# Experts' columns in blocks of 1024, a token's weight applied when a result is added to it, and another order of the products in a piece

## The chip, the core and the metric

The kernel runs on one core of a Trainium2 chip. The metric is device time in microseconds (us), the median of several runs. TensorE (PE) multiplies, ScalarE (ACT) and VectorE (DVE) evacuate PSUM and prepare operands, SyncE (SP) issues the loads. Times with five or six digits in the rows below are places in the profiled execution, counted from its start.

## The reference

The program is a two-layer encoder on 256 tokens of 1024 columns. Each layer is a mixer and then a feed-forward part; in the second layer that part is a mixture of eight experts of width 3584. The change touches the experts alone:

```python
def swiglu(h, w1, w3, w2):
    return (jax.nn.silu(h @ w1) * (h @ w3)) @ w2

def moe_swiglu(h, router_w, w1, w3, w2):
    t = h.reshape(B * L, D)
    logits = (t @ router_w).astype(jnp.float32)
    top_val, top_idx = lax.top_k(logits, TOP_K)
    top_w = jax.nn.softmax(top_val, axis=-1)
    combine = jnp.einsum('tk,tke->te', top_w, jax.nn.one_hot(top_idx, N_EXPERTS))
    out = jnp.zeros_like(t)
    for e in range(N_EXPERTS):
        out = out + combine[:, e:e + 1] * swiglu(t, w1[e], w3[e], w2[e])
    return out.reshape(B, L, D)
```

## The kernel before

Every float32 product is made of float32r products. A weight piece r (4 KB a partition, 512 KB in all, one load on SP's queue) is split into H, a copy by ACT (L319, tile wh), and L = r - H, a subtraction by DVE (L320, tile wl); activations are split in the same way. A product then takes three matrix products: high times H, high times L, low times H. H and L have four slots each. When PE takes a piece (`take`), the split of the piece three further on is put into the queues of ACT and DVE, where it waits until PE has done with the slot. Loaded pieces wait in some twenty further tiles.

The experts run one after the other. At most 128 tokens of an expert are gathered by products with a one-hot matrix (tiles gx). The 3584 columns of w1 and w3 are worked in seven blocks of 512. A block is, in PE's order: the product with w1 (L1884 to L1886, 24 matrix products into one PSUM tile `mo`), the transposes of the former block's activations (L1844, PSUM tile `maT`), the product with w3 (24), and the former block's product with w2 (L1813 to L1815, 24, into two PSUM tiles `my`). Behind that, ACT computes the block's Silu from w1's tile (L1894) and DVE multiplies by w3's tile (L1895). PE, ACT and DVE all work in the order in which the program issues (`by_hand`).

PSUM has eight tiles of one bank: four with the tag `pw` (all of `mo`), two `pg` (`my`) and two `pl` (transposes, gathers, scatters). Tiles of a tag are handed out in turn, and a tile's next writer waits until the readers of its former content are done.

When the last block of an expert is through w2, its result is scaled by the tokens' weights (`weighted`: ACT L1822 writes ywH, DVE L1823 writes ywL); the weights in slot order (`wsl`) come from products of the one-hot matrix (L1799). `scatter` brings the result back to token order in four units of two products (L1836, L1837, PSUM tile `sc`), each added to the sum by DVE (L1838). Scatter and gather are issued between the rows of the running products: a call of `pump` lets a waiting unit go when its count is down.

A piece of w1 or w3 holds two rows of 128 by 512 columns (2 KB runs in memory); a piece of w2 holds one row of 1024 columns (4 KB runs).

Of the kernel before, what the change touches and what calls it, by code (L numbers as in the profile page):

```python
# [10 lines left out]
F32 = mybir.dt.float32  # L11
# [4 lines left out]
OP = mybir.AluOpType  # L16
# [16 lines left out]
def _constants():  # L33
    """Masks and identities, all set by the shapes alone."""
# [43 lines left out]
def _build(ctx, tc, nc, A, out, dbg, upto):  # L78
# [6 lines left out]
    # a pool for all phases (tags m..), and two (tags g.. and l..) of the mixers that the experts' replace  # L85
# [19 lines left out]
    # slots of a pool's tags; the last character of a tag is its size: 4, 2, 1 KB, h(alf), s(mall)  # L105
# [14 lines left out]
    # work that is issued between the pieces of a long product  # L120
# [41 lines left out]
    # ------------------------------------------------------------------ constants and small inputs  # L162
# [70 lines left out]
    # rotary angles: the argument reduced to [-pi, pi], cos from the half angle  # L233
# [26 lines left out]
    # lambda of the differential attention, and rows that depend on parameters alone  # L260
# [28 lines left out]
    # the slots of the weights' pieces: the pools that hold them, each with its number  # L289
# [14 lines left out]
    # instructions of a critical chain, behind which the engines' other work is queued  # L304
# [8 lines left out]
    def split(r, early=None, lows=None):  # L313
        """Two float32r parts whose sum is r, in the slots of the weights or of another tag."""
# [42 lines left out]
    def load_ahead(tags):  # L357
        """The next pieces of the plan, into tiles of their own tags (or the weights' slots)."""
# [5 lines left out]
    def lend(until):  # L364
        """The tiles of the pieces loaded ahead also hold later pieces, in the same order, up to the until-th piece."""
# [19 lines left out]
    def pieces(name, rows, step=1, k=0, ahead=True):  # L385
        """(k, H, L) over the contraction, from row k; work of the sides is issued every step rows."""
# [7 lines left out]
    def mm_nat(o, k, H, L, xs, tb, last, parts=(0, 1)):  # L394
        """Activations stationary: [128 tokens, columns] += ."""
# [7 lines left out]
    def proj_nat(name, xs, rows=KD, n=512):  # L403
        """[tokens, n] for both token blocks."""
# [6 lines left out]
    def proj_first(name, xs, stages):  # L411
        """proj_nat of the first block: token block 1 becomes ready after token block 0."""
# [14 lines left out]
    def proj_T(name, n, xs, step=1, o=None, k0=0, rows=KD):  # L427
        """[n columns, 256 tokens] in chunks of 128 columns, two to a bank; k0, rows: a part of the contraction."""
# [35 lines left out]
    def adaln(todo, every):  # L464
        """Vectors (layer, index) of the modulation as columns [128, 8], a piece of the weights at a time."""
# [11 lines left out]
    def sums(half):  # L477
        """Columns half * 4.. of the modulation's first two vectors: pieces on PE or on DVE, and the end."""
# [107 lines left out]
    def row_of(col, name):  # L586
        """A [128, 8] column vector as a row of 1024 on every partition."""
# [9 lines left out]
    def norm_T(l, n_i, sc_i, sh_i, keep=None):  # L597
        """The modulated norm of x, transposed, as two float32r parts [128, 2, 8, 128]: tiles, and a step a block."""
# [19 lines left out]
        def xn(tb, at=512):  # L618
            """Scaled on DVE as far as column at, beyond on ACT."""
# [16 lines left out]
        def hf(tb, q, dve=2):  # L636
            """The first columns on DVE, the others on ACT."""
# [18 lines left out]
    def warm(n):  # L656
        """Products that nothing reads, to keep PE's clock up while it waits for a chain of other engines."""
# [5 lines left out]
    def rstd2(ss, name):  # L663
        """(ss[:, 0] + ss[:, 1] + eps) ** -0.5, of squares that were divided by 1024"""
# [5 lines left out]
    def to_T(src_cols, ks, dst, scale=None, tags=("pl",)):  # L670
        """Transposed, scaled by a column and split: src_cols(tb, k) -> [128 tokens, 128]; dst = (H, L). In steps."""
# [18 lines left out]
    def residual(ys):  # L690
        """The steps of x += g * rmsnorm(y); ys[tb] are the halves of y, [128, 512] each."""
# [28 lines left out]
    def transition(r, grow, n, then):  # L720
        """The residual r, and the norm n as far as block 0's transposes and then(), in the order in which the data comes."""
# [21 lines left out]
    def after(res, norm):  # L743
        """The steps of a norm that follows a residual, for a product that begins with token block 0."""
# [1276 lines left out]
```

## Time and profile before

| what | us |
|---|---|
| median of three timed runs | 1929.86 |
| lowest and highest of them | 1929.14, 1938.19 |
| span of the profiled execution, first to last instruction | 1935.8 |
| PE busy | 1886.1 (97%) |
| DVE busy | 1598.8 (83%) |
| ACT busy | 1329.8 (69%) |

The page lists no time of the profiled execution besides its span, which lies among the three timed runs. Matrix products overlap in the records: a product of 512 columns is listed with about 0.39 us, but one starts every 0.23 us; the distance of starts is what counts. The experts run from 933.7 us to the end.

### The profile page before, as it was taken

The numbers are of one execution on the slowest core, as the hardware profiler recorded it, in microseconds if no ns is written. First come the engines' busy times: TensorE is split into PE (matmuls) and PEld (weight loads), VectorE is DVE, ScalarE is ACT, GpSimd is POOL, SyncE is SP. The second block draws the span as 40 slices with busy tenths as digits, with TensorE's granted clock in tenths as the row PEclk, the third lists the DMA queues.
The fourth block names the chain that finished last, engine by engine and source line by source line (L and its number), as shares of the span: only waits on it lengthen the run. The fifth ranks groups of instructions, "written<-read, shape, count | busy, mean of one in ns | idle before, by whom it ended". The sixth has DMA issues, their size and how long they took to land.

```text
span 1935.8 us, 32487 instructions
## 1 busy us (share of the span) xinstructions
PE 1886.1 (97%) x12232; PEld 1583.8 (82%) x12232; DVE 1598.8 (83%) x1993; ACT 1329.8 (69%) x1874; POOL 30.1 (2%) x54
## 2 busy tenths in 40 slices
PE   7999999999999999999999999999999999999997
PEld 6987788799878878787788888888888888888885
DVE  6887876677756887766899988999889999899997
ACT  4785566643346873665777787777887778877775
POOL 1000000000000000000000000000000000000000
PEclk9999999999999999999999999999999999999999
DMA  9545755478874557558799999999999999999992
GB/s 326 162 129 174 221 175 182 154 251 268 283 227 125 148 155 219 185 184 322 267 342 351 337 349 344 367 370 356 355 338 369 369 354 368 335 358 373 360 322 107
DMA packets 258018, 531.30 MB, mean 274 GB/s; under 512 B 22126, under 2 KB 45116, under 8 KB 257852
## 3 DMA queue, kind: packets, MB, share of 16 engines
q1 hardware_dynamic: 257500, 528.99, 79.7%
q8 instruction: 98, 1.61, 0.3%
q14 instruction: 68, 0.56, 0.1%
q0 software_dynamic: 192, 0.07, 0.0%
q10 hardware_dynamic: 160, 0.07, 0.0%
HBM read 528.02 MB, written 1.05 MB: 273 GB/s over the span
## 4 chain that ended last, share of the span: by engine, by line
PE 75%; DMA 9%; DVE 6%; ACT 6%; issue 2%; SPq 1%; POOL 0%; DVEq 0%; ACTq 0%; POOLq 0%
PE mo L1884 11%; PE mo L1886 11%; PE mo L1885 11%; PE my L1813 5%; PE my L1814 5%; PE my L1815 5%; DMA raw<-in_adaln_w 4%; PE pn L398 4%; PE pn L401 4%; PE pn L399 4%; DMA raw<-in_ffn_w 2%; DVE wl L320 2%; ACT wh L319 2%; PE pt L437 2%; PE pt L438 2%
## 5 line engine op out<-in xcount | busy, mean ns | idle before, releaser
L320 DVE TENSOR_TENSOR wl<-raw,wh 128x1024 fp32r<-128x1024 f32 (+1 forms) x893 | 1076.3, 1222 | 166.3 <-ACT wh L319 126.8
L319 ACT CAST wh<-raw 128x1024 fp32r<-128x1024 f32 (+1 forms) x893 | 931.8, 1053 | 380.0 <-PE mo L1886 96.9
L1884 PE MATMUL mo<-wh,gx 128*128 128x512 f32 x896 | 357.0, 398 | 0.0
L1885 PE MATMUL mo<-wl,gx 128*128 128x512 f32 x896 | 351.0, 392 | 0.0
L1886 PE MATMUL mo<-wh,gx 128*128 128x512 f32 x896 | 350.9, 392 | 0.0
L1886 PEld LDWEIGHTS mo<-wh,gx 128*128 128x128 f32 x896 | 168.2, 188 | 38.6 <-ACT gx L1785 1.2
L1884 PEld LDWEIGHTS mo<-wh,gx 128*128 128x128 f32 x896 | 168.4, 188 | 34.7 <-ACT gx L1785 0.6
L1885 PEld LDWEIGHTS mo<-wl,gx 128*128 128x128 f32 x896 | 168.5, 188 | 34.5 <-DVE wl L320 0.2
L1813 PE MATMUL my<-wh,aTm 128*128 128x512 f32 x448 | 175.9, 393 | 0.0
L1814 PE MATMUL my<-wl,aTm 128*128 128x512 f32 x448 | 175.3, 391 | 0.0
L1815 PE MATMUL my<-wh,aTm 128*128 128x512 f32 x448 | 175.1, 391 | 0.0
L437 PE MATMUL pt<-xH,wh 128*128 128x256 f32 x576 | 165.7, 288 | 0.0
L438 PE MATMUL pt<-xH,wl 128*128 128x256 f32 x576 | 163.1, 283 | 2.1 <-DVE wl L320 2.1
L439 PE MATMUL pt<-xL,wh 128*128 128x256 f32 x576 | 162.9, 283 | 0.0
L398 PE MATMUL pn<-wh,xH 128*128 128x512 f32 x352 | 150.0, 426 | 0.0
L401 PE MATMUL pn<-wh,xL 128*128 128x512 f32 x352 | 139.4, 396 | 0.0
L399 PE MATMUL pn<-wl,xH 128*128 128x512 f32 x352 | 139.4, 396 | 0.0
L450 DVE SCALAR_TENSOR_TENSOR acc<-raw,scol,acc 128x512 f32<-128x512 f32 x140 | 104.7, 748 | 39.9 <-DMA raw<-in_adaln_w 38.0
L438 PEld LDWEIGHTS pt<-xH,wl 128*128 128x128 f32 x576 | 110.4, 192 | 2.8 <-DVE wl L320 2.5
L437 PEld LDWEIGHTS pt<-xH,wh 128*128 128x128 f32 x576 | 110.4, 192 | 0.3
L439 PEld LDWEIGHTS pt<-xL,wh 128*128 128x128 f32 x576 | 110.4, 192 | 0.0
L1815 PEld LDWEIGHTS my<-wh,aTm 128*128 128x128 f32 x448 | 84.1, 188 | 18.9
(450 smaller groups left out, 2518.2 us busy)
## 6 DMA issues: line engine op xcount, KB each, us to landing
raw<-in_moe_w SPq DMA_DIRECT2D x672, 512.0 KB, 5.3
raw<-in_w_in SPq DMA_DIRECT2D x128, 512.0 KB, 3.8
raw<-in_adaln_w SPq DMA_DIRECT2D x80, 512.0 KB, 4.6
raw<-in_ffn_w SPq DMA_DIRECT2D x66, 512.0 KB, 4.8
raw<-in_w_branch SPq DMA_DIRECT2D x24, 512.0 KB, 4.2
rawe<-in_adaln_w SPq DMA_DIRECT2D x16, 512.0 KB, 7.9
raw<-in_w_out SPq DMA_DIRECT2D x16, 512.0 KB, 4.9
x<-in_x SPq DMA_DIRECT2D x2, 512.0 KB, 6.9
```

What stands on the lines that cost most here:

```text
L319: S.copy(H, r)
L320: low = lambda: tt(L, r, H, op=OP.subtract)
L398: mm(o, xH[:, tb, k, :], H, start=k == 0, stop=False)
L437: mm(d, H[:, cs], xH[:, :, k, :], start=k == 0 and c % 2 == 0, stop=False, skip_group_check=True)
L438: mm(d, L[:, cs], xH[:, :, k, :], start=False, stop=False, skip_group_check=True)
L439: mm(d, H[:, cs], xL[:, :, k, :], start=False, stop=k == KD - 1, skip_group_check=True)
L1813: mm(y[hf], aT[:, 0, k, :], H[:, c], start=b == 0 and k == 0, stop=False)
L1814: mm(y[hf], aT[:, 0, k, :], L[:, c], start=False, stop=False)
L1815: mm(y[hf], aT[:, 1, k, :], H[:, c], start=False, stop=b == nb - 1 and k == 3)
L1884: mm(q, gH[:, k, :], H, start=k == 0, stop=False)
L1885: mm(q, gH[:, k, :], L, start=False, stop=False)
L1886: mm(q, gL[:, k, :], H, start=False, stop=k == KD - 1)
```

## The change

Blocks are now 1024 columns wide (three of 1024 and one of 512 per expert). A piece of w1 or w3 is one row of 1024 columns. A block's w1 and w3 take two PSUM tiles each, and within a piece the order is: high and low times H for the first half, high and low times H for the second, then high times L for both. `turned` transposes two tiles, `gated` computes two Silus and two products. `parted` splits the result without weights; the weight is a column operand of the addition, which becomes a SCALAR_TENSOR_TENSOR, and the products for `wsl` are gone. `pump` is called once per row and half. The numbers that say how long the lent tiles hold loaded pieces (`lend`) follow the new order.

```diff
+    EB = [(c, min(1024, DE - c)) for c in range(0, DE, 1024)]
...
-        nb = DE // 512
+        nb = len(EB)
...
-                ws = ps("ws", [P, 2])
...
-                        mm(ws[:, j:j + 1], hot[tb][:, j, :].bitcast(F32), combk[:, tb, e:e + 1],
-                           start=tb == 0, stop=tb == 1)
...
-                    act(yH[:, c], y[hf], AF.Copy, scale=wcol)
-                    stt(yL[:, c], y[hf], wcol, yH[:, c], op0=OP.mult, op1=OP.subtract)
+                    S.copy(yH[:, c], y[hf])
+                    tt(yL[:, c], y[hf], yH[:, c], op=OP.subtract)
...
-                        tt(acc[tb][:, c], acc[tb][:, c], o, op=OP.add)
+                        stt(acc[tb][:, c], o, combk[:, tb, e:e + 1], acc[tb][:, c], op0=OP.mult, op1=OP.add)
...
-                        q = ps("mo", [P, 512], "pw")
+                        o[w] = [ps("mo", [P, 512], "pw") for _ in subs]
...
-                                mm(q, gH[:, k, :], H, start=k == 0, stop=False)
-                                mm(q, gH[:, k, :], L, start=False, stop=False)
-                                mm(q, gL[:, k, :], H, start=False, stop=k == KD - 1)
-                                pump()
+                                for q, j in zip(o[w], subs):
+                                    c = slice(512 * j, 512 * j + 512)
+                                    mm(q, gH[:, k, :], H[:, c], start=k == 0, stop=False)
+                                    mm(q, gL[:, k, :], H[:, c], start=False, stop=False)
+                                for q, j in zip(o[w], subs):
+                                    c = slice(512 * j, 512 * j + 512)
+                                    mm(q, gH[:, k, :], L[:, c], start=False, stop=k == KD - 1)
+                                    pump()
...
                     def gated():
-                        act(t, o[0], AF.Silu)
-                        tt(t, t, o[1], op=OP.mult)
+                        for j in subs:
+                            act(t[j], o["moe_w1"][j], AF.Silu)
+                            tt(t[j], t[j], o["moe_w3"][j], op=OP.mult)
```

Three places show how the change moves instructions. The first is ACT's queue where expert 0's result is complete, behind the first block of expert 1. `my_1` and `my_2` are the result's halves, `mo` the PSUM tiles of the block's w1. Before:

```order
L319 CAST wh_316_11367<-raw1_5_9924 128x1024
L1822 ACTIVATE ywH_1_11377<-my_1_10417,wsl_1_10147 128x512
L1822 ACTIVATE ywH_1_11377<-my_2_10418,wsl_1_10147 128x512
L1894 ACTIVATE ma_8_11330<-mo_15_11224 128x512
L319 CAST wh_317_11387<-raw1_6_9926 128x1024
```

And now:

```order
L319 CAST wh_324_11455<-raw_383_11453 128x1024
L1821 CAST ywH_1_11465<-my_1_10602 128x512
L1821 CAST ywH_1_11465<-my_2_10603 128x512
L1901 ACTIVATE ma_8_11415<-mo_15_11217 128x512
L1901 ACTIVATE ma_9_11416<-mo_16_11218 128x512
L319 CAST wh_325_11479<-raw_384_11477 128x1024
```

There are two Silus instead of one, behind the same two copies. `mo_15` and `mo_16` are the w1 tiles of this block, `mo_17` and `mo_18` its w3 tiles; with four `pw` tiles handed out in turn, the next block's w1 tiles, `mo_19` and `mo_20`, take the places of `mo_15` and `mo_16`. Before, one block took two tiles and the next block's w1 the places of the block before the last.

The second place is PE's queue in the w1 product of the following block, at the scatter of expert 0 (`sc_18` and `sc_19` are its second and third unit, `maT_8` and `maT_9` the transposes of the former block):

```order
L1893 MATMUL mo_19_11475<-wl_328_11516,gx_3_10144 128x512
L1834 MATMUL sc_18_11564<-ywH_1_11465,hT_1_10146 128x512
L1835 MATMUL sc_18_11564<-ywL_1_11466,hT_1_10146 128x512
L1893 MATMUL mo_20_11476<-wl_328_11516,gx_3_10144 128x512
...
L1893 MATMUL mo_19_11475<-wl_329_11528,gx_3_10144 128x512
L1834 MATMUL sc_19_11580<-ywH_1_11465,hT_1_10146 128x512
L1835 MATMUL sc_19_11580<-ywL_1_11466,hT_1_10146 128x512
L1893 MATMUL mo_20_11476<-wl_329_11528,gx_3_10144 128x512
L1844 MATMUL maT_8_11585<-cc_79,ma_8_11415 128x128 x4
L1844 MATMUL maT_9_11593<-cc_79,ma_9_11416 128x128 x4
```

Three of the four scatter units now stand ahead of the transposes, and the transposes fill two `pl` tiles, those that `sc_18` and `sc_19` held. Before, all four units stood behind the transposes, which filled one tile.

The third is DVE's queue at the same place, with the additions of those units (`acc`) between the subtractions (`wl`):

```order
L320 TENSOR_TENSOR wl_330_11540<-raw_389_11537,wh_330_11539 128x1024
L1836 SCALAR_TENSOR_TENSOR acc_25_11008<-sc_17_11548,combk_9931,acc_25_11008 128x512
L320 TENSOR_TENSOR wl_331_11556<-raw_390_11553,wh_331_11555 128x1024
L1836 SCALAR_TENSOR_TENSOR acc_25_11008<-sc_18_11564,combk_9931,acc_25_11008 128x512
L320 TENSOR_TENSOR wl_332_11572<-raw_391_11569,wh_332_11571 128x1024
L1836 SCALAR_TENSOR_TENSOR acc_26_11009<-sc_19_11580,combk_9931,acc_26_11009 128x512
L1847 TENSOR_TENSOR aTm_8_11590<-maT_8_11585,aTm_8_11590 128x512
L1847 TENSOR_TENSOR aTm_9_11598<-maT_9_11593,aTm_9_11598 128x512
```

The addition that frees `sc_19` for `maT_9` stands behind two subtractions and two other additions that begin after the first unit.

## Rows read from the trace of the kernel before

**Rows 1.** Busy time by stage: us, PE PEld DVE ACT POOL, clock, DMA share, GB/s.

```profile
500.00:600.00 100.00, 91.65 (x447) 74.30 (x446) 64.02 (x83) 47.45 (x69) 3.12 (x6) 0.98 0.68 217
...
1200.00:1300.00 100.00, 100.00 (x450) 82.00 (x449) 93.38 (x86) 77.69 (x82) 0.00 (x0) 1.00 1.01 365
...
1500.00:1600.00 100.00, 100.00 (x450) 81.92 (x449) 93.44 (x88) 78.61 (x84) 0.00 (x0) 1.00 0.99 362
```

**Rows 2.** Waits from 950 to 1920 us: us in total, times, longest.

```profile
ACT wh L319 <- PE mo L1886: 96.2, 285, 0.8
...
DVE wl L320 <- DMA raw<-in_moe_w: 9.3, 35, 1.2
...
ACT wh L319 <- DMA raw<-in_moe_w: 1.6, 5, 0.3
...
PEld mo L1885 <- DVE wl L320: 0.2, 1, 0.2
```

**Rows 3.** Timeline at the border of two blocks: start, us, engine, line.

```profile
1246.66 0.39 PE L1815 MATMUL my<-wh,aTm 128*128 128x512 f32 x1
...
1247.08 1.05 ACT L319 CAST wh<-raw 128x1024 fp32r<-128x1024 f32 x1 [0.31 <-PE my L1815]
...
1248.02 0.39 PE L1815 MATMUL my<-wh,aTm 128*128 128x512 f32 x1
1248.04 0.59 ACT L1894 ACTIVATE ma<-mo 128x512 f32<-128x512 f32 x1
1248.24 0.40 PE L1884 MATMUL mo<-wh,gx 128*128 128x512 f32 x1
...
1248.53 1.04 ACT L319 CAST wh<-raw 128x1024 fp32r<-128x1024 f32 x1
...
1251.03 0.39 PE L1884 MATMUL mo<-wh,gx 128*128 128x512 f32 x1
...
1253.52 0.39 PE L1886 MATMUL mo<-wh,gx 128*128 128x512 f32 x1
```

**Rows 4.** Timeline where an expert's result is complete.

```profile
1315.88 0.39 PE L1815 MATMUL my<-wh,aTm 128*128 128x512 f32 x1
1315.91 1.26 ACT L1822 ACTIVATE ywH<-my,wsl 128x512 fp32r<-128x512 f32 x2
1316.11 0.40 PE L1884 MATMUL mo<-wh,gx 128*128 128x512 f32 x1
...
1317.06 0.59 ACT L1894 ACTIVATE ma<-mo 128x512 f32<-128x512 f32 x1
```

**Rows 5.** Timeline at the end: additions free PSUM tiles that PE waits for.

```profile
1921.75 1.36 DVE L1838 TENSOR_TENSOR acc<-acc,sc 128x512 f32<-128x512 f32 x2
...
1922.49 0.50 PE L1836 MATMUL sc<-ywH,hT 128*128 128x512 f32 x1
...
1922.83 0.40 PE L1837 MATMUL sc<-ywL,hT 128*128 128x512 f32 x1
```

**Rows 6.** ACT's timeline at the first Silu.

```profile
949.50 1.03 ACT L319 CAST wh<-raw 128x1024 fp32r<-128x1024 f32 x1
950.55 1.28 ACT L1894 ACT_TABLE_LOAD   x1
951.84 0.60 ACT L1894 ACTIVATE ma<-mo 128x512 f32<-128x512 f32 x1
```

**Rows 7.** Groups from 950 to 1900 us: busy us, mean ns, idle before.

```profile
L320 DVE TENSOR_TENSOR wl<-raw,wh 128x1024 fp32r<-128x1024 f32 x650 | 781.2, 1222 | 72.5 <-ACT wh L319 36.9 <-DMA raw<-in_moe_w 9.3
...
L1823 DVE SCALAR_TENSOR_TENSOR ywL<-my,wsl,ywH 128x512 fp32r<-128x512 f32 x14 | 9.8, 743 | 0.0
...
L1799 PE MATMUL ws<-combk,hot 128*128 128x1 f32 x32 | 4.0, 229 | 0.0
```

**Rows 8.** The chain that ended last: start, us, what.

```profile
1253.91 0.44 PE maT L1844 x4
...
1414.62 0.34 PE ws L1799 x4
```

**Rows 9.** PE's timeline in the first layer's feed-forward part.

```profile
575.22 0.40 PE L1503 MATMUL po<-wh,gT 128*128 128x512 f32 x1
...
577.79 0.39 PE L1505 MATMUL po<-wh,gT 128*128 128x512 f32 x1
```

More of the change, by code (lines that the diff above doesn't have):

```diff
@@ L1804, in gather, with parted @@
                     S.copy(hT[j], o[:, j])
-                S.copy(wsl, ws)
             def down(y, b, aT, then=None):
-                for k, H, L in pieces("moe_w2", 4):
+                rows = EB[b][1] // P
+                for k, H, L in pieces("moe_w2", rows):
                     if k == 1 and then:
                         then()
+                    a = aT[k // 4][:, :, k % 4, :]
                     for hf in range(2):
                         c = slice(hf * 512, hf * 512 + 512)
-                        mm(y[hf], aT[:, 0, k, :], H[:, c], start=b == 0 and k == 0, stop=False)
-                        mm(y[hf], aT[:, 0, k, :], L[:, c], start=False, stop=False)
-                        mm(y[hf], aT[:, 1, k, :], H[:, c], start=False, stop=b == nb - 1 and k == 3)
-            def weighted(y, wcol):
+                        mm(y[hf], a[:, 0], H[:, c], start=b == 0 and k == 0, stop=False)
+                        mm(y[hf], a[:, 0], L[:, c], start=False, stop=False)
+                        mm(y[hf], a[:, 1], H[:, c], start=False, stop=b == nb - 1 and k == rows - 1)
+            def parted(y):
                 yH = tl("ywH", [P, D], "m4", F32R)
@@ L1832, in scatter, with turned @@
                         o = ps("sc", [P, 512])
-                        for e in es:
-                            yH, yL = yws.pop(e) if hf == tb == 1 else yws[e]
-                            hT = of[e][1]
-                            mm(o, hT[:, tb, :], yH[:, c], start=e == es[0], stop=False)
-                            mm(o, hT[:, tb, :], yL[:, c], start=False, stop=e == es[-1])
-                        tt(acc[tb][:, c], acc[tb][:, c], o, op=OP.add)
-            def turned(t):
-                q = ps("maT", [P, 4, P])
-                for k in range(4):
-                    nc.tensor.transpose(q[:, k, :], t[:, k * P:k * P + P], ident)
-                aT = tl("aTm", [P, 2, 4, P], "m4", F32R)
-                S.copy(aT[:, 0], q)
-                tt(aT[:, 1], q, aT[:, 0], op=OP.subtract)
-                return aT
+                        yH, yL = yws.pop(e) if hf == tb == 1 else yws[e]
+                        hT = of[e][1]
+                        mm(o, hT[:, tb, :], yH[:, c], start=True, stop=False)
+                        mm(o, hT[:, tb, :], yL[:, c], start=False, stop=True)
+                        stt(acc[tb][:, c], o, combk[:, tb, e:e + 1], acc[tb][:, c], op0=OP.mult, op1=OP.add)
+            def turned(ts_):
+                aTs = []
+                for t in ts_:
+                    q = ps("maT", [P, 4, P])
+                    for k in range(4):
+                        nc.tensor.transpose(q[:, k, :], t[:, k * P:k * P + P], ident)
+                    aT = tl("aTm", [P, 2, 4, P], "m4", F32R)
+                    S.copy(aT[:, 0], q)
+                    tt(aT[:, 1], q, aT[:, 0], op=OP.subtract)
+                    aTs.append(aT)
+                return aTs
             def end(e, b, aT, every, then=None):
@@ L1855, in end @@
                 if b == nb - 1:
-                    yws[e] = weighted(ys[e], of[e][2])
-                    return Side(scatter((e,), every), 1)
+                    yws[e] = parted(ys[e])
+                    return Side(scatter(e, every), 1)
             of, ys, yws, prev = {}, {}, {}, None
@@ L1863, in experts @@
                 for b in range(nb):
-                    if e % 2 and b == 4 and e + 1 < NE:
+                    if e % 2 and b == 2 and e + 1 < NE:
                         more = Side(gather(e // 2 + 1, 4), 1)
@@ L1867, in experts @@
                         more.drain("gather")
-                    if not acc and b == 5:
+                    if not acc and b == nb - 1:
                         acc.extend(tl("acc", [P, D], "l4") for _ in range(2))
@@ L1871, in experts @@
                             G.memset(t, 0.0)
-                    o = []
                     final = e == NE - 1 and b == nb - 1
+                    subs = range(EB[b][1] // 512)
+                    o = {}
                     for w in ("moe_w1", "moe_w3"):
-                        q = ps("mo", [P, 512], "pw")
-                        for k0 in range(0, KD, 2):
-                            if e == b == 0 and w == "moe_w1":
+                        o[w] = [ps("mo", [P, 512], "pw") for _ in subs]
+                        k = -1
+                        while k < KD - 1:
+                            if e == b == 0 and w == "moe_w1" and k % 2:
@@ L1878, in experts @@
                                 next(first)
                                 next(first)
-                                if k0 == KD - 2:
+                                if k == KD - 3:
                                     Side(first, 8)
                             gH, gL = of[e][0]
-                            for k, H, L in take(w, not (final and w == "moe_w3" and k0 >= KD - 4)):
-                                mm(q, gH[:, k, :], H, start=k == 0, stop=False)
-                                mm(q, gH[:, k, :], L, start=False, stop=False)
-                                mm(q, gL[:, k, :], H, start=False, stop=k == KD - 1)
-                                pump()
@@ L1888, in experts @@
-                        o.append(q)
+                            for k, H, L in take(w, not (final and w == "moe_w3" and k >= KD - 5)):
+                                for q, j in zip(o[w], subs):
[6 more added lines that the diff above has]
+                                    pump()
@@ L1900, in experts @@
                         gated()
-                    if e == NE - 1 and b == nb - 3:
+                    if e == NE - 1 and b == nb - 2:
                         grow = row_of(gcol, "grow")
```

18 lines of the change are left out of this document (8 added, 10 removed).

## The prediction

> **What bounds the kernel now.** I read the busy time by stage first. The change touches only the experts, from 933.7 us on. There PE is busy for all of every 100 us at full clock, DVE for 93, ACT for 79, and the DMA engines for about all of it; in the first layer's feed-forward part, which the change leaves alone, PE has gaps [rows 1]. Three resources are near their limit, so the waits decide which one sets the pace. In the whole stage PE waited 0.2 us for a split piece, while ACT waited 96 us for PE to give a slot back; the loads kept DVE waiting 9.3 us and ACT 1.6 [rows 2]. ACT and DVE follow PE. PE's queue is the path: whatever adds a wait to PE is added to the time, and a faster load, copy or addition gives nothing as long as PE does not wait for it.
>
> What PE's path is made of is seen at a border of two blocks [rows 3]. A product starts every 0.23 us: 12 products from 1248.24 to 1251.03 take 2.79 us, the next 11 take 2.49, or 0.2264 each. So a new product runs 12 x 0.2264 = 2.72 us worth of work in 2.79, that is 0.07 us is lost at its start, and the rest goes at one spacing whichever operand is stationary.
>
> **The change, part by part.**
>
> *Wider rows in memory.* The 8 x 7 x 12 = 672 pieces stay 512 KB each. The page has no row for 4 KB runs alone. Upper bound of the gain: everything that was waited for a load, 9.3 + 1.6 = 10.9 us, if it lay on PE's path; lower bound 0. It lies on DVE and ACT, who are ahead of PE, so I take 0. The cover is PE's own work; if PE became faster the loads would be next, at 0.99 to 1.01 of the DMA engines' time [rows 1]. The Trainium skill ("Perfetto Trace Analysis", DMA Optimizations) says that larger transfers, 4 KB in place of 2 KB, can raise throughput much where DMA is the limit; the DMA share would agree, the waits do not.
>
> *The products.* Their number is the same, 8 x 7 x 72 = 4032 in all, 2688 of them of w1 and w3, and so is that of the transposes. An expert starts 12 products (w1, w3, w2 in four blocks) instead of 21; 8 x 9 x 0.07 = 5.0 us less. Bounds: 0, if the loss comes back with the alternation of two PSUM tiles; or a slower spacing throughout, as in the feed-forward part, where 11 steps from 575.22 to 577.79 take 0.2336 each [rows 9]. Against the mean of the first 23 steps here, (2.79 + 2.49) / 23 = 0.2296, that is 0.004 on 2688 products of w1 and w3, 10.8 us more. I take 5.0 less, since new products are nearest to what both stages show.
>
> *The weights' products.* 4 pairs of experts, two groups each of 0.34 us on the chain [rows 8], all 32 records of the group [rows 7]: 4 x 2 x 0.34 = 2.7 us less, on PE's path. Bounds 0 (if the transposes next to them wait as long anyway) and 2.7.
>
> *A wait at the border of blocks.* This is the main term. All four `pw` tiles are now one block's; the next block's first product needs the tile that the Silu reads, and the Silu stands in ACT's queue behind w2's product. Today the Silu starts at 1248.04, because the copy before it starts only when PE gives a slot back (1247.08, after the product of 1246.66), and ends at 1248.63; PE's next product starts at 1248.24 and needs nothing from it [rows 3]. Now it must wait. What such a wait costs beyond the reader's end is seen at the end of the kernel: the addition ends at 1921.75 + 0.68 = 1922.43, the product that needs its tile starts at 1922.49, and the following one 0.34 later instead of 0.23 [rows 5]. So: 1248.63 + 0.06 - 1248.24 + 0.11 = 0.56 us. The second Silu ends 0.49 later (the distance from the first to the copy behind it, 1248.04 to 1248.53), and its tile is needed two products, 0.57 us, after the first: no second wait. The tiles turn so that the border from the 512 block to the next expert is free; two borders per expert (second and third block, third and fourth) cost this: 16 x 0.56 = 9.0 us. Bounds: 0.39, the bare overlap, to 0.62: 6.2 to 9.9.
>
> *The border at which an expert's result is complete.* Between an expert's first and second block ACT first copies the former expert's result, so the Silu starts only at 1317.06 and ends at 1317.65, while PE goes on at 1316.11 [rows 4]. The wait is 1.54 + 0.06 + 0.11 = 1.71 us, for experts 1 to 7: 12.0 us. Bounds: 1.54 to 1.8, 10.8 to 12.6. For expert 0 the table load, 1.28, and the Silu, 0.60, follow a copy of 1.03 [rows 6]; that copy starts about when PE begins its last row of 6 products (1.38 us) and the wait is 1.03 + 1.28 + 0.60 - 0.2 - 1.38 + 0.17 = 1.5 us; bounds 0 and 1.5. The 0.2 is that H is now given back two products earlier, so that the copy three rows ahead starts 0.2 to 0.3 before PE begins a row. This extra lead of ACT and DVE is all that the order within a piece gives; as PE did not wait for them, it is worth 0.
>
> *The transposes behind the scatter.* `maT_9` takes the tile of the third scatter unit. Count from PE's start on the row with the first unit. PE needs three rows of 6 products and three units of 2, 24 x 0.228, and four transposes of 0.44 in all [rows 8]: it wants the tile at 5.9. DVE ends the subtraction ahead of the first addition at about 2.1 (copy from -0.25 to 0.8, then 1.22 [rows 7]); then come addition, subtraction, addition, subtraction, addition. An addition with a weight does not exist before; nearest is the same operation with a PSUM input, 0.74 [rows 7]. So 2.1 + 3 x 0.74 + 2 x 1.22 = 6.8, and with the 0.06 and 0.11 a wait of 1.1 us, for 7 experts 7.7 us. Bounds 0, if DVE is ahead, and 1.5, if it comes late out of the double block of multiplications: 0 to 10.5. Queued behind `maT_9` on PE is the whole of w3; nothing else waits.
>
> *The rest.* Two multiplications and two transposed copies come at once on DVE and ACT instead of one; the lead of the splits covers them, and PE's new waits lengthen it. The additions are 0.06 longer on DVE, 28 of them off PE's path; four at the end cost 0.2, and the plain copies of the result give about as much back. Zero.
>
> *Sum*: 9.0 + 12.0 + 1.5 + 7.7 - 5.0 - 2.7 = 22.5 us more. On the profiled execution, 1935.8, that is 1958.3; this execution is 5.9 above the median of the three runs, so for a median I predict 1929.9 + 22.5 = 1952 us.
>
> The Trainium skill ("Perfetto Trace Analysis", Optimizing Tensor Performance, Matmuls) asks that independent products rotate through different PSUM banks, so that reading one overlaps the next. The kernel before does so, the trace agrees (the 1248.24 product needs no reader), and the change gives it up: by the rule slower, as in the sum.
>
> **The rivals.**
>
> *The waits do not show.* If ACT reached the Silus before PE is through w2, the three wait terms vanish and 5.0 + 2.7 are left: 1922 us, within 0.5%. For it: ACT has 21 of 100 us free. Against: the order puts the Silu behind a copy that PE itself releases in the last row but one.
>
> *Products get closer.* The new order seldom repeats a stationary operand. If that took the spacing of w1's and w3's products from 0.2296 to 512 columns at 2.4 GHz (the granted clock is 1.00), 0.2133, it would give 2688 x 0.0163 = 43.8 us, in place of the 5.0: 1929.9 + 27.5 - 43.8 = 1914 us, faster. It decides from 0.014 us a product. Against: in the 2.49 us of equal steps the stationary operand changes at two of three steps and stays at the third, with no difference. The Trainium skill ("TensorE: Matmul & The Clock Gate", Back-to-back issue gap) gives 0.216 us for 512 columns; no row here shows that.
>
> *Loads were the bound after all.* All 10.9 us come back, the waits stay: 1941 us, 0.6% slower.
>
> **How the numbers follow.** 0.5% is 9.6 us, about what a measurement of this kernel can tell from no change. The forecast's case, 1940 to 1966, has 0.70; the waits hidden wholly or mostly, 1922 to 1939, 0.18; closer products 0.09; loads 0.03, mostly just slower. Faster 0.10, same 0.19, slower 0.71. The terms' own bounds: at least 6.2 + 10.8 - 5.0 - 2.7 = 9, at most 9.9 + 12.6 + 1.5 + 10.5 + 10.8 - 2.7 = 43. The range 1930 to 1966 leaves out the closer products, the lower half of the hidden waits, and the top of the last sum.
>
> **What would show it.** In the profile after, PE's idle time or the distance of starts at the first w1 product of a block should name the Silu's line: 0.4 to 0.6 us at 16 places, 1.6 to 1.8 at 7; the transposes behind a scatter should wait about 1 us for an addition; starts inside a product should keep 0.226 to 0.235. The prediction is wrong if PE runs through those borders, or if the spacing inside w1 and w3 moves by over 0.005.

## The result, and the profile after

The changed kernel takes 1954.32 us (median of 4 runs, 1953.64 to 1956.04) against 1929.5 us for the kernel before (median of 4 runs, 1929.13 to 1938.19): ratio 1.0115, 95% interval 1.0092 to 1.0139 (the quotient of the two medians, 1.0129, lies inside it). It is slower, and within 3 us of the forecast.

Busy time by stage in the changed kernel (PE, its loads of stationary operands as PEld, DVE, ACT, POOL, clock, DMA share, GB/s), which answers to [rows 1]:

```profile
1200.00:1300.00 100.00, 97.90 (x436) 79.18 (x435) 91.11 (x85) 76.34 (x81) 0.00 (x0) 1.00 0.96 354
1500.00:1600.00 100.00, 98.19 (x441) 79.83 (x440) 90.97 (x85) 76.39 (x82) 0.00 (x0) 1.00 0.97 362
```

PE, full before, now idles for 2 of every 100 us at the same clock, and DVE, ACT and the loads all do a little less per 100 us. Nobody is fuller than before: a wait has been added. Its name stands in the waits from 950 to 1935 us (us in total, times, longest), as in [rows 2]:

```profile
ACT wh L319 <- PE mo L1890: 92.3, 285, 0.8
...
PEld mo L1889 <- ACT ma L1901: 28.2, 40, 2.2
...
PE mo L1889 <- ACT ma L1901: 15.1, 24, 1.8
...
DVE wl L320 <- DMA raw<-in_moe_w: 11.8, 45, 1.2
ACT wh L319 <- DMA raw<-in_moe_w: 3.8, 12, 0.3
PEld maT L1844 <- DVE acc L1836: 3.6, 7, 0.5
...
PE maT L1844 <- DVE acc L1836: 2.0, 7, 0.3
```

L1889 is the first product of a row's half of w1 or w3, L1901 the Silu, L1836 the scatter's addition. PE waits for the Silu at 24 places, which are all the borders that the prediction counted (16, 7 and 1), and for the addition at 7. The totals of PE are too small (a product's record is listed longer than the distance of starts), so the sizes below are taken from starts. The timeline at an ordinary border, which answers to [rows 3]:

```profile
1242.55 1.06 ACT L319 CAST wh<-raw 128x1024 fp32r<-128x1024 f32 x1 [0.30 <-PE my L1814]
1243.51 1.08 ACT L1901 ACTIVATE ma<-mo 128x512 f32<-128x512 f32 x2
...
1243.49 0.39 PE L1814 MATMUL my<-wh,aTm 128*128 128x512 f32 x1
1244.15 0.50 PE L1889 MATMUL mo<-wh,gx 128*128 128x512 f32 x1 [0.28 <-ACT ma L1901]
1244.49 0.40 PE L1890 MATMUL mo<-wh,gx 128*128 128x512 f32 x1
```

The first of the two Silus begins at 1243.51 behind a copy that PE released late, and ends some 0.59 later, at 1244.10. PE starts at 1244.15, 0.66 after w2's last product instead of 0.227, and the next product follows 0.34 later, as in [rows 5]. The border behind which an expert's result is complete, which answers to [rows 4]:

```profile
1329.41 1.07 ACT L1821 CAST ywH<-my 128x512 fp32r<-128x512 f32 x2
1330.36 1.10 ACT L1901 ACTIVATE ma<-mo 128x512 f32<-128x512 f32 x2
...
1329.39 0.39 PE L1814 MATMUL my<-wh,aTm 128*128 128x512 f32 x1
1331.03 0.50 PE L1889 MATMUL mo<-wh,gx 128*128 128x512 f32 x1 [1.25 <-ACT ma L1901]
```

Here the two copies go first, and PE loses 1.64 - 0.23 = 1.41 and 0.1 behind it. Expert 0's first border, which answers to [rows 6]:

```profile
953.46 2.01 ACT L319 CAST wh<-raw 128x1024 fp32r<-128x1024 f32 x2
955.49 1.28 ACT L1901 ACT_TABLE_LOAD   x1
956.78 1.09 ACT L1901 ACTIVATE ma<-mo 128x512 f32<-128x512 f32 x2
...
957.43 0.50 PE L1889 MATMUL mo<-wh,gx 128*128 128x512 f32 x1 [1.81 <-ACT ma L1901]
```

PE's product ahead of it starts at 955.23, so 2.20 - 0.23 = 1.97 us are lost here.

The second transposes behind the additions of a scatter:

```profile
1341.83 0.75 DVE L1836 SCALAR_TENSOR_TENSOR acc<-sc,combk,acc 128x512 f32<-128x512 f32 x1
1342.49 1.22 DVE L320 TENSOR_TENSOR wl<-raw,wh 128x1024 fp32r<-128x1024 f32 x1
1343.63 0.74 DVE L1836 SCALAR_TENSOR_TENSOR acc<-sc,combk,acc 128x512 f32<-128x512 f32 x1
...
1343.54 0.60 PE L1844 MATMUL maT<-cc,ma 128*128 128x128 f32 x4
1344.42 0.66 PE L1844 MATMUL maT<-cc,ma 128*128 128x128 f32 x4 [0.28 <-DVE acc L1836]
```

The third addition ends at 1344.37, and the tile's transposes start at 1344.42 instead of 1343.98.

Because the stages ahead differ by some us between executions, the experiments are also compared by the experts' stage, from the start of the first w1 product to that of the last w2 product in the profiled execution: 986.2 us before (933.69 to 1919.93), 1009.1 after (927.26 to 1936.35), 22.9 us more. One thing disturbs this comparison. In five of the runs below PE's granted clock is 0.5, the lower of its two levels (1.2 GHz), for some us at or near the stage's start, and a product of 512 columns then starts every 0.427 us. The first 96 products of w1 and w3 take 1.5 us longer by it with the early Silu (926.39 to 929.80) and with the spread scatter (926.98 to 930.40) than with the early Silu and the later scatter together, where the clock stays at 1.00; the later scatter alone loses 0.5 us, and the old order, against the changed kernel, nothing. In the run with one pair of tiles it is 1.5 us, right behind 3.37 us in which no product started. PE was busy for 4.06 of 5 us shortly before the fall in the spread run, and for as much in the run with both edits, where no fall came; why it fell stays open.

### The profile page after: what moved, and what is told of

Read it like the earlier page. It is cut to its first block, busy times and chain, and to the rows that moved or that the text cites. A ratio compares the mean times of both kernels' runs of the same rounds, so it can differ in the third digit from the quotient of the medians.

```text
span 1951.8 us, 32414 instructions
## 1 busy us (share of the span) xinstructions
PE 1888.1 (97%) x12200; PEld 1576.3 (81%) x12200; DVE 1599.4 (82%) x1993; ACT 1328.5 (68%) x1870; POOL 29.7 (2%) x54
## 4 chain that ended last, share of the span: by engine, by line
PE 74%; DMA 8%; ACT 8%; DVE 8%; issue 2%; POOL 0%; SPq 0%; DVEq 0%; ACTq 0%; POOLq 0%
PE mo L1889 10%; PE mo L1890 10%; PE mo L1893 10%; PE pn L398 5%; PE pn L401 4%; DVE wl L320 4%; PE pn L399 4%; PE my L1812 4%; PE my L1814 4%; PE my L1813 4%; ACT wh L319 3%; DMA raw<-in_adaln_w 3%; DMA raw<-in_ffn_w 2%; PE pt L437 2%; PE pt L438 2%
## 5 line engine op out<-in xcount | busy, mean ns | idle before, releaser
L1889 PE MATMUL mo<-wh,gx 128*128 128x512 f32 x896 | 357.3, 399 | 15.1 <-ACT ma L1901 15.1
L1893 PE MATMUL mo<-wl,gx 128*128 128x512 f32 x896 | 294.7, 391 | 0.0
L1889 PEld LDWEIGHTS mo<-wh,gx 128*128 128x128 f32 x896 | 168.3, 188 | 62.1 <-ACT ma L1901 28.2
L450 DVE SCALAR_TENSOR_TENSOR acc<-raw,scol,acc 128x512 f32<-128x512 f32 x140 | 104.7, 748 | 39.4 <-DMA raw<-in_adaln_w 37.5
```

Source lines behind the costliest of these rows:

```text
L1889: mm(q, gH[:, k, :], H[:, c], start=k == 0, stop=False)
L1893: mm(q, gH[:, k, :], L[:, c], start=False, stop=k == KD - 1)
```

## The experiments

**The Silu earlier.** If the Silu's place in ACT's queue is the cause, moving it into w3's product must remove all 24 border waits.

```diff
+                                if w == "moe_w3" and k in (3, 5) and (k - 3) // 2 in subs:
+                                    j = (k - 3) // 2
+                                    act(t[j], o["moe_w1"][j], AF.Silu)
...
                         for j in subs:
-                            act(t[j], o["moe_w1"][j], AF.Silu)
                             tt(t[j], t[j], o["moe_w3"][j], op=OP.mult)
```

> The changed kernel, with the Silus issued earlier: ACT gets them behind the fourth and the sixth row of w3's product instead of behind w2's product; the multiplications stay where they were. My theory is that PE waits at a block's first w1 product because the Silu stands late in ACT's queue. In the changed kernel's trace the 23 borders behind a w2 product cost 17.0 us at the first distance of starts and 2.6 us at the one behind it, and the border of expert 0's first two blocks 2.1 us, 21.7 us in all. By the theory all of this goes: 1954.3 - 21.7 = 1932.6 us, and the distance from w2's last product to the next w1 product is 0.227 us at every border. Rival: the two tiles per product are the cause (PSUM tiles change hands between ACT and PE whatever the order), then the borders keep at least 0.4 us each and the time stays above 1945. Second rival: the Silus in the middle of w3 delay the copies of the split behind them, and PE waits there for H instead; then the time stays near 1954, and the waits name L319.

Measured: 1942.99 us (before on this chip 1931.89), ratio 1.0055 (1.0042 to 1.0069); stage 998.9. The mechanism held: w2's last product and the next w1 product are 0.227 apart at all 30 such pairs. The size did not: only 10.2 of the 21.7 us came back, and neither rival tells why. Of the missing 11.5 us, 1.5 are the lower clock. PE's timeline shows where nearly all the rest is:

```profile
1336.17 0.39 PE L1893 MATMUL mo<-wl,gx 128*128 128x512 f32 x1
1336.89 0.66 PE L1844 MATMUL maT<-cc,ma 128*128 128x128 f32 x4 [0.33 <-DVE acc L1836]
1338.68 0.66 PE L1844 MATMUL maT<-cc,ma 128*128 128x128 f32 x4 [1.14 <-DVE acc L1836]
```

Now both transposes wait, by 0.49 and 1.30 over the undisturbed 0.23 and 0.11, 1.8 us at each of 7 places instead of 0.45. The two waits were not separate: while PE stood at the border, DVE caught up with its additions. Of the 1.5 us saved at a border, 1.35 were paid again in the same product.

**The scatter later, alone and with the early Silu.**

```diff
-                        yield 5 * every if tb == hf == 0 else every
+                        yield 8 * every if tb == hf == 0 else every
```

> The changed kernel, with the first scatter unit held back until 16 calls of pump instead of 10, so that all four units stand behind the transposes as in the kernel before. Theory: the second transpose tile waits only because the addition of the third unit is late; 7 places at (0.55 - 0.11) + about 0.05, 3.6 us in the changed kernel's trace. Expected 1954.3 - 3.6 = 1950.7 us, and no distance over 0.2 us between transposes. Rival: the tile is handed out late in any order (then the units wait for the transposes' readers instead, ACT L1846 and DVE L1847), and the time stays at 1954.

Measured: 1951.6 us, ratio 1.0096 (1.008 to 1.0112); stage 1006.2, 2.9 less than the changed kernel's, with no distance over 0.2 us between transposes: near the 3.6 us expected, of which 0.5 are lost to the lower clock.

With both edits:

> Both of the two edits: the Silus in the middle of w3's product, and the four scatter units behind the transposes. If the two costs are separate they add: 1954.3 - 21.7 - 3.6 = 1929.0 us, the time of the kernel before less nothing that can be measured. By the forecast's term of 5.0 us for fewer product starts, and 2.7 us for the weights' products, it would be 1929.5 - 7.7 = 1922; the changed kernel's trace says that only transposes, not product starts, have a loss behind them, so I expect 1926 to 1930. Rival: without PE's waits the splits or the loads lose their lead and become the bound, then 1935 or more with waits of PE for L319 or L320.

Measured: 1932.75 us, ratio 1.0005 (0.9992 to 1.0019); stage 986.35. Both waits are gone, and the kernel is level with the one before: the two edits together take back the whole loss, 22.7 of 22.9 us of the stage, though alone they took 10.2 and 2.9. The second scatter unit now waits a little, 0.46 us behind the product ahead of it instead of 0.23:

```profile
1330.93 0.40 PE L1893 MATMUL mo<-wl,gx 128*128 128x512 f32 x1
1331.38 0.50 PE L1834 MATMUL sc<-ywH,hT 128*128 128x512 f32 x1
1331.72 0.39 PE L1835 MATMUL sc<-ywL,hT 128*128 128x512 f32 x1
```

**The order of products.** It was undone in the changed kernel, and done alone in the kernel before. In the changed kernel:

```diff
                                 mm(q, gH[:, k, :], H[:, c], start=k == 0, stop=False)
-                                mm(q, gL[:, k, :], H[:, c], start=False, stop=False)
...
-                                mm(q, gH[:, k, :], L[:, c], start=False, stop=k == KD - 1)
+                                mm(q, gH[:, k, :], L[:, c], start=False, stop=False)
+                                mm(q, gL[:, k, :], H[:, c], start=False, stop=k == KD - 1)
```

> The changed kernel with the products of a piece in the order of before: for each half high times H, high times L, low times H. By my theory the order of stationary and moving parts is worth nothing: 1954 us, within 2 us. Rival: the alternation of the stationary part makes the products closer and hides a loss elsewhere; undone it would cost 0.003 us or more on each of 2688 products, 8 us or more, 1962 us. Rival on the other side: H is given back two products later, and ACT and DVE fall behind: some us more, with PE waiting for L319 or L320.

Measured: 1957.21 us, ratio 1.0123 (1.0105 to 1.0141), not told apart from the changed kernel's 1.0115 by the times. The stage is 1013.9, 4.8 longer, and the trace names it:

```profile
1084.84 0.60 PE L1844 MATMUL maT<-cc,ma 128*128 128x128 f32 x4
1086.25 0.66 PE L1844 MATMUL maT<-cc,ma 128*128 128x128 f32 x4 [0.82 <-DVE acc L1836]
```

The second transposes wait 0.98 us instead of 0.45 at 7 places (3.7 us), and three gathers by 0.44 (1.3 us). The distances inside products are the same (0.2325 and 0.227 us, see below). So the new order does nothing for PE's spacing; by giving H back earlier it lets DVE come to the additions sooner, which is worth something only where PE waits for one.

In the kernel before:

```diff
                                 mm(q, gH[:, k, :], H, start=k == 0, stop=False)
-                                mm(q, gH[:, k, :], L, start=False, stop=False)
-                                mm(q, gL[:, k, :], H, start=False, stop=k == KD - 1)
+                                mm(q, gL[:, k, :], H, start=False, stop=False)
+                                mm(q, gH[:, k, :], L, start=False, stop=k == KD - 1)
```

> The kernel before with the new order of a row's products alone (high times H, low times H, high times L). PE never waits for a split there, so an earlier release of H is worth nothing: theory 1.000, and a mean distance of starts within 0.001 us of that before. Rival: the stationary part that no longer repeats makes products closer; 0.0163 us on 2688 products would be 43.8 us, 0.977; a tenth of that, 4 us, would still show as 0.998.

Measured: 1933.23 us, ratio 1.001 (0.9995 to 1.0024). Nothing, as expected; the rival of closer products is excluded.

**Wider rows.** The loads of the kernel before with 4 KB runs:

```diff
-                    add(w, lambda k0, kn, w=w, e=e, b=b: kview(A[w][0, e], b * 512, 512, k0, kn), KD, 512)
+                    add(w, lambda k0, kn, w=w, e=e, b=b: kview(A[w][0, e], min(b // 2 * 1024, 2560), 1024, k0 + b % 2, 1).rearrange(
+                        "p k (h n) -> p (k h) n", h=2), KD, 512)
```

> The kernel before with loads of w1 and w3 whose runs in memory are 4 KB: a piece is loaded as one row of 1024 columns instead of two rows of 512, the same bytes in all but for the last block of an expert, and used as if it were the old piece, so the products are made with other weights. Theory: the loads are ahead of PE, 0 us, ratio 1.000. Rival: the loads were the bound in part, up to 10.9 us less, ratio 0.994, with fewer waits of DVE and ACT for loads.

Measured: 1930.07 us, ratio 1.000 (0.9986 to 1.0014). Its waits for loads, against 9.3 and 1.6 us in [rows 2]:

```profile
DVE wl L320 <- DMA raw<-in_moe_w: 11.1, 35, 1.2
...
ACT wh L319 <- DMA raw<-in_moe_w: 4.0, 10, 0.8
```

They are no fewer, and nobody on the path waits for them. The Trainium skill ("Perfetto Trace Analysis", DMA Optimizations) promises its gain from larger transfers where DMA is the limit; a DMA share of 1.0 in [rows 1] did not make it one here, since the split of each piece was still ahead of PE.

**The weights applied later.** This part of the change alone, in the kernel before: no products for `wsl`, a plain split of the result, and the weight as an operand of the addition.

```diff
-                        mm(ws[:, j:j + 1], hot[tb][:, j, :].bitcast(F32), combk[:, tb, e:e + 1],
-                           start=tb == 0, stop=tb == 1)
...
-                        tt(acc[tb][:, c], acc[tb][:, c], o, op=OP.add)
+                        stt(acc[tb][:, c], o, combk[:, tb, e:e + 1], acc[tb][:, c], op0=OP.mult, op1=OP.add)
```

> The kernel before with one part of the change: the products of the weights are gone, the result is split without a weight, and the addition multiplies by it. Theory: the two groups of products on PE's queue at four places go, 2.7 us less by the forecast's term, and 3.3 us less by the difference of the starts around them in the two traces; the longer addition is hidden. So 0.998 of the time before. Rival: the longer additions hold PSUM tiles that PE waits for, and the gain is lost.

Measured: 1927.22 us (before 1932.27), ratio 0.9966 (0.9942 to 0.9989); stage 982.0, 4.2 less. The gain is there and somewhat larger: by the starts around them the products gave 3.3 us, as the second estimate had it, and three waits of the one-hot transposes (0.50 us each by the starts in the kernel before) went too, 4.8 in all. That they went because `ws` no longer holds one of the two `pl` tiles fits the order of the tiles, but was not tried by itself. A new wait of PE for a split, 0.6 us at 951.6, takes the rest back.

**The tile's turn in narrow blocks.** Does the wait need wide blocks at all?

```diff
+                        if w == "moe_w3":
+                            skipped = [ps("skip", [P, 512], "pw") for _ in range(2)]
```

> The kernel before, in blocks of 512, with two pw tiles skipped behind each block, so that the next block's w1 product gets the very tile that the Silu of this block reads, as in the changed kernel. Nothing else is moved. Theory: the wait at a border comes from the turn of the tiles and the Silu's place alone, and not from the width of a block: 47 ordinary borders at 0.53 us, 7 behind which a result is split at 1.5 us, and expert 0's first at 2.1 us, 24.9 + 10.5 + 2.1 = 37.5 us more, ratio 1.0195. Rival: the wait needs two Silus and two multiplications at once; then the ratio stays within 1.003.

Measured: 1932.28 us, ratio 1.0008 (0.9992 to 1.0023). In its trace no product waits for a Silu. So the next block's product did not get the Silu's tile, it seems because tiles that nothing writes were given no place, and the run says nothing on the theory. The same question with one pair of tiles kept throughout:

```diff
-                        q = ps("mo", [P, 512], "pw")
+                        if w not in pair:
+                            pair[w] = ps("mo", [P, 512], "pw")
+                        q = pair[w]
```

> The kernel before, in blocks of 512, with one pair of PSUM tiles kept for all w1 and w3 products of the experts, so that a block's first w1 product needs the tile that the former block's Silu reads. In the run with two skipped tiles this was not so: a tile that nothing writes took no place, and the products went on through four tiles. Theory: the wait comes from the tile and the Silu's place alone: 47 ordinary borders at 0.53 us, 7 behind which a result is split at 1.5, expert 0's first at 2.1, 24.9 + 10.5 + 2.1 = 37.5 us more, ratio 1.0195, with starts 0.66 us apart at the ordinary borders. Rival: the wait needs the two Silus and two multiplications of a wide block; then the ratio stays within 1.003.

Measured: 1974.71 us (before 1932.91), ratio 1.0211 (1.019 to 1.0232); stage 1028.6, 42.4 more. Narrow blocks, the same border:

```profile
1250.86 0.39 PE L1815 MATMUL my<-wh,aTm 128*128 128x512 f32 x1
1250.88 0.59 ACT L1897 ACTIVATE ma<-mo 128x512 f32<-128x512 f32 x1
...
1251.53 0.51 PE L1887 MATMUL mo<-wh,gx 128*128 128x512 f32 x1 [0.28 <-ACT ma L1897]
1251.87 0.39 PE L1888 MATMUL mo<-wl,gx 128*128 128x512 f32 x1
```

One Silu and one multiplication give the same 0.67 and 0.34. What the width does is use up the spare pair of tiles; the wait itself comes from the tile and the Silu's place. Of the 4.9 us above the expected 37.5, 2.4 lie at the 8 longer borders: 7 of 1.82 us instead of 1.64, and expert 0's of 3.37 instead of 2.20; 1.5 are the lower clock behind that border.

**Towards the best version.** The early Silu, with scatter units two rows apart:

```diff
-                        yield 5 * every if tb == hf == 0 else every
+                        yield 10 * every if tb == hf == 0 else 2 * every
```

> The changed kernel with the Silus in the middle of w3's product, and the scatter units from the third row of w3's product on, two rows apart. With all four units right behind the transposes, the trace still had 7 places at which the second unit waited (0.463 instead of 0.227 us, and 0.11 behind it), 2.4 us. Theory: DVE, which needs 1.22 us of a row's 1.38 for the subtraction, can't take an addition of 0.74 in every row; in every second row it comes 0.4 us late instead of 0.6 and has had two rows more behind the transposes, so the unit's tile is free: 2.4 us less than with the units one row apart, 1932.75 - 2.4 = 1930.3, ratio 0.9993. Rival: the wait is moved to a later unit or to the gather, and the time stays.

Measured: 1929.74 us (before 1932.91), ratio 0.9984 (0.9969 to 0.9999); stage 985.4. The units' waits are gone, yet the stage is only 1.0 shorter, not 2.4. The lower clock hides it: the first 96 products took 1.5 us longer than in the run it is compared with, and behind them the stage is 2.5 shorter, as the theory has it. Then the remaining two places, with the kernel before plus the later weights beside it on the same chip:

```diff
+                if pr:
+                    yield 2 * every
                 o = ps("hTp", [P, 2, 2, P])
...
+                                one = e == b == 0 and w == "moe_w1"
...
+                                for q, c in cs if one else ():
+                                    mm(q, gL[:, k, :], H[:, c], start=False, stop=k == KD - 1)
+                                    pump()
```

> The changed kernel with the Silus in the middle of w3's product, the scatter units two rows apart from the third row of w3's product on, and two more places mended: the transposes of the one-hot matrices wait two rows longer (before, three waits of 0.44 us for the readers of the block's transposes), and in the very first w1 product both low times H come last, as high times L did in the kernel before (five waits of about 0.32 us for the second gathered part). Theory: what remains is the kernel before without the weights' products: 1.3 + 1.6 = 2.9 us less than the run with the spread scatter, ratio 0.9984 - 0.0015 = 0.997, and an experts' stage of 982.5 us from the first w1 product to the last w2 product. Rival: the blocks of 1024 have a loss or a gain of their own, then the stage ends away from the 982.0 us of the kernel before with the weights applied later.

> The kernel before with only the weights applied later, once more, on the chip of the run with all waits moved, to set the two beside each other. Theory: blocks of 1024 columns with a row of 4 KB give nothing of their own once their waits are gone, so the two are within 0.1%: 0.997 here too. Rival: the wide blocks gain by fewer product starts, 5.0 us by the forecast's term; then all waits moved is at 0.994 and this one at 0.997.

Measured: all waits moved 1926.38 us, ratio 0.9972 (0.9953 to 0.999), stage 981.1; the weights alone 1926.57 us (before 1932.53), ratio 0.9965 (0.9951 to 0.9979), stage 982.0. Both beat the kernel before and the changed one, and they are level. With all waits moved, PE is full again:

```profile
1200.00:1300.00 100.00, 100.00 (x452) 82.23 (x451) 93.26 (x87) 76.64 (x81) 0.00 (x0) 1.00 0.98 364
1500.00:1600.00 100.00, 100.00 (x448) 82.09 (x447) 92.62 (x88) 77.76 (x83) 0.00 (x0) 1.00 0.97 366
```

So the blocks of 1024 columns have neither a loss nor a gain of their own that shows: the stages differ by 0.9 us, and 0.6 of that is the wait for a split in the kernel with the weights alone. All that the change gives is the weights' products, and all that it costs is three kinds of waits: for the Silus, of the second transposes for the scatter's additions, and in the very first w1 product for the second gathered part. The fourth kind that was moved here, that of the one-hot transposes, the kernel before has too.

## Why the prediction was right

The forecast of 22.5 us more stands beside 22.9 in the stage and 24.8 between the medians. Its terms, measured by the excess of start distances in the changed kernel's trace (except where another run is named):

| term | predicted | measured |
|---|---|---|
| 16 ordinary borders | +9.0 | 16 x (0.441 + 0.103) = +8.7 |
| 7 borders behind a complete result | +12.0 | 7 x (1.41 + 0.10) = +10.6 |
| expert 0's first border | +1.5 | 1.97 + 0.10 = +2.1 |
| 7 second transposes | +7.7 | 7 x (0.45 + 0.05) = +3.5 |
| fewer product starts | -5.0 | 0 |
| no products for the weights | -2.7 | -3.3; the waits of the one-hot transposes beside them, gone in the run of the weights alone, are there as before |
| first w1 product +0.9, gathers and all smaller differences +0.4 | none | +1.3 |
| sum | +22.5 | +22.9 |

**The border of blocks**, the main step, was right in place, count and size. The first Silu ends and PE starts 0.05 later, the second Silu costs nothing more, and both removing the wait (the early Silu) and making it elsewhere (one pair of tiles) moved the time as the step says. The Trainium skill's rule on rotating PSUM banks ("Perfetto Trace Analysis", Optimizing Tensor Performance, Matmuls) points the same way, and the run with one pair gives it a price, 42.4 us for 55 borders.

**The border behind a complete result** was 0.2 too long per place. The prediction took two scaled copies from [rows 4] (1.15 us from the first to the Silu); plain copies take 0.95 (1329.41 to 1330.36).

**Expert 0's border** was 0.6 too short. The prediction let the last copy ahead of the table load start 0.2 before PE's last row. Two copies stand there without a gap, 953.46 to 955.47, so the last starts at about 954.4, while PE's last row begins at 955.23 + 0.23 - 1.38 = 954.1: 0.5 later than assumed.

**The second transposes** were right in mechanism and mis-sized, 0.5 instead of 1.1. The sum 2.1 + 3 x 0.74 + 2 x 1.22 added durations, but DVE's instructions follow each other closer than they last: from addition to subtraction 1341.83 to 1342.49 is 0.66, from subtraction to addition 1342.49 to 1343.63 is 1.14. Five such steps are 0.4 shorter, which is most of the difference. That the additions came as early as that was itself owed to PE's wait at the border, as the early Silu showed; the terms of the sum were not independent.

**Fewer product starts, -5.0, is the step that failed.** In [rows 3] the first 12 products took 0.07 longer than 12 equal steps, and the prediction put this to the product's start. The first product of each row of a wide block in the changed kernel:

```profile
1245.67 0.39 PE L1889 MATMUL mo<-wh,gx 128*128 128x512 f32 x1
...
1247.05 0.39 PE L1889 MATMUL mo<-wh,gx 128*128 128x512 f32 x1
...
1248.41 0.39 PE L1889 MATMUL mo<-wh,gx 128*128 128x512 f32 x1
...
1249.77 0.40 PE L1889 MATMUL mo<-wh,gx 128*128 128x512 f32 x1
...
1251.18 0.39 PE L1889 MATMUL mo<-wh,gx 128*128 128x512 f32 x1
...
1252.56 0.39 PE L1889 MATMUL mo<-wh,gx 128*128 128x512 f32 x1
...
1253.92 0.39 PE L1889 MATMUL mo<-wh,gx 128*128 128x512 f32 x1
```

A row is six products on one piece. The rows last 1.38, 1.36, 1.36, 1.41, 1.38, 1.36: the slow row comes back with the fifth, in the middle of a product (the first, from 1244.15, is 1.52 with the 0.11 behind the wait, 1.41 without). Over all products between 960 and 1900 us, waits left out and counted from the first w1 product, the first 11 steps of every 24 average 0.2325 and the other 13 0.227, in both kernels. 24 products are four pieces. In the kernel before that was also one product of w1, w3 or w2, which is why it looked like a start. The number of such turns, 4032 / 24 = 168, is the same in both, so nothing was saved.

That the total came out so near is partly luck: 5.0 us too much gain and 4.2 us too much for the transposes offset each other, and the smaller misses of the table, between -1.4 and +1.3, come to -0.4.

**The zeros** held for the wider rows, in the times and in the waits for loads, and for the longer additions, for which no product waits in the run with the weights applied later. For the order within a piece the zero holds in the kernel before and for the distance of products. It does not hold in the changed kernel: the prediction gave ACT and DVE's extra lead no worth because PE did not wait for them, but it had itself put a wait for DVE's additions into the sum, and there the lead saves 4.8 us of the stage. The rivals fell: PE did not run through the borders, products are no closer in either kernel, and the loads were not the bound. For the rival of closer products, the Trainium skill ("TensorE: Matmul & The Clock Gate", Back-to-back issue gap) has 0.216 us for 512 columns as the gap of a product taken alone, and 0.131 for a sustained stream of weight loads and products; no run here shows less than 0.226 as the usual distance in such a stream, and the measurement decides.

## What to carry to other kernels

Before you merge tiles or widen a block, count how many PSUM tiles are left in turn: with none to spare, the time from the next writer to the last reader of the former content is on the path, and that reader's place in its engine's queue sets the price. The cure that worked here, at all 24 places, was to issue the reader earlier, when its input was complete. Where one engine waits at two places for engines that run behind, the waits are not a sum: taking one away can move most of it to the other (here 1.35 of 1.5 us), so both have to be moved before either is worth its size.

## What the runs showed that was not expected

The distance between products has two levels that come back every four pieces: 0.2325 us for 11 steps, then 0.227 for 13, in products of 24 and of 48 alike. The slots of H and L also turn by four, so the place in SBUF may be behind it. The first layer's feed-forward part points the same way: the steps of its last product go from 0.2267 to 0.2334 us at 564.23 us in the kernel before, with the step to the 217th of 264 matrix products, where the stationary operand passes from tiles with the tag `l4` to tiles with the tag `g4`. But some ten steps behind that product's earlier pauses are slow too, and no run moved a tile to try this; it stays open. At 11 x 0.0055 = 0.06 us for each of 168 turns it is some 10 us of this kernel, more than any version here won (6.2 between the medians).

A DMA share of 1.0 with 365 GB/s was not a bound: the kernel with waits moved keeps PE full at a share of 0.98, and the kernel before gained nothing from wider rows.
